# First stage of a gated retention and attention block: half of the modulation summed on VectorE, the keys' banks held open over two chunks

## The chip, the cores and the metric

One NeuronCore of one Trainium2 chip runs the whole block in one launch. The metric is the device time of one execution in microseconds (us). Engines are named as in the profile: PE is TensorE's matrix multiply, PEld its weight load, DVE is VectorE, ACT is ScalarE, POOL is GpSimd, SP issues most of the DMAs.

## The reference, cut to what matters

The block computes, for a sequence of 512 tokens and a model width of 2048:

```
mod = silu(c) @ w_ada + b_ada                      # c: one vector of 2048; w_ada: 2048 x 6144
shift, scl, gate = split(mod, 3)
h = rmsnorm(x) * g_norm * (1 + scl) + shift        # 512 x 2048
(r_q, r_k, r_v, r_g, n_q, n_kc, n_vc, n_ks, ...) = split(h @ w_in)
...
x = rmsnorm(x + gate * (merged @ w_out)) * g_final
```

The keys of the attention half (n_ks, n_kw) and the queries are rotated by position: `x * cos + rot(x) * sin`. Everything behind `h @ w_in` needs h, and h needs the sum over all 2048 rows of `w_ada` for its own columns. The change touches this first stage only.

## The kernel before, in words

The 2048 columns of h are made in eight chunks of 256 (j = 0 to 7, two k-tiles of 128 each). For a chunk the 2 x 256 columns of `w_ada` for shift and scale are loaded as eight items of 512 KB (each holds two k-tiles of the sum). TensorE multiplies them with silu(c): two k-tiles per item, with 32 columns of weights, so that four such products lie side by side in the array (`ada_batch`, L353, output tile `pa`). ScalarE copies the sums to SBUF (`ada_rows`, L358, tile `rows`), four small matmuls turn them into columns (`cols_mm`, L336, tile `misc`), three small VectorE operations make the two factors of each column (tile `sh`, L372 to L374), and `cols_h` applies them: VectorE scales (L381), ScalarE rounds to the high part `hhi` (L382), VectorE takes the rest `hlo` (L383). Every product with h is made of three matmuls (hi x hi, hi x lo, lo x hi), and the weights are split likewise: `whi` on ScalarE (L269), `wlo` on VectorE (L270).

As soon as two k-tiles of h exist, two groups of columns of `w_in` use them: the group "kc" keeps four PSUM banks open over all chunks (class `Group`, L453, tile `g`), 24 matmuls per chunk, and the group "k" (the keys) takes 24 matmuls per chunk in two banks that take turns (`k_step`, L907, tile `g` too); after each chunk VectorE adds every finished bank to an SBUF sum `kacc` (L913). After the last chunk the keys are rotated in place (`rope`, L529 to L533). The position tables cos and sin are made on VectorE in small operations that are spread over the chunks (`rope_tables`, L503 to L522).

The order on each engine is the order of the program text; nothing is moved by a scheduler. Steps of the two groups lie in a list `todo`, and `pop(room)` emits some of them between the modulation's batches. A step can only stand behind the chunk whose k-tiles it reads. `early_splits` splits weights ahead, up to an item that `lim` names. The loads go out on SP in the order of `plan`, each into the next free one of nine slots (seventeen up to chunk 2), and wait there until the slot's last reader is done.

After the first stage the next group is "v" (matmuls of L453 again, between them the products `phid` of the compression, L642), then the queries and the rest of `w_in`.

Of the kernel before, what the change touches and what calls it, by code (L numbers as in the profile page):

```python
# [85 lines left out]
def block_kernel(ctx: ExitStack, tc: tile.TileContext, t_in, out):  # L86
    nc = tc.nc
# [17 lines left out]
    def sbank(name):  # L105
        return bank("pss", 2, name)
# [66 lines left out]

    plan = []


    BATCH = [[2, 2, 2, 2]] * 2 + [[4, 4]] * 6
    for j in range(8):
        for u in range(8):
            plan.append(("a", j, u))  # L180
            if (j, u) == (0, 3):
                plan.append(("w", "in", 0, 0))
        plan += [("w", "in", g, j) for g in range(2) if j or g]
    n_start = len(plan)
    for g in range(2, NG):
        for s in range(8):
# [11 lines left out]
        for s in range(8):  # L198
            plan.append(("w", "out", j, s))

    SRC = {"a": "w_ada", "in": "w_in", "c": "w_c1", "g": "w_gate", "up_r": "w_ur", "up_n": "w_un", "out": "w_o"}
    raws, splits = {}, {}
    loaded = [0]
    w_idx = [i for i, it in enumerate(plan) if it[0] == "w"]
    w_ord = {i: n for n, i in enumerate(w_idx)}
    parked = {}
    split_ptr = [0]
# [44 lines left out]
    def take(i):  # L252

        if i not in raws:
            load(i)
        slots.append(held.pop(i))
        return raws.pop(i)
# [55 lines left out]
    def rstd_rows():  # L313
        prs = sbank("prs")
        for t in range(NT):
            c = slice(t * P, (t + 1) * P)
            nc.tensor.matmul(prs[:, c], ones, rtmp[:, 2, c], start=t == 0, stop=t == NT - 1, skip_group_check=True)
        nc.vector.tensor_copy(rstd, prs)


    def xn(j, us):

        for u in us:
            kk = 2 * j + u
            h = xT[kk // 8][:, kk % 8, :]
            nc.vector.tensor_tensor(h, h, rstd, op=OP.mult)
# [12 lines left out]
    pa = {}  # L339

    def ada_batch(idx, j, s0, n):


        load(idx + n - 1)
        per = 2 if j else 4
        w = 1024 // per
        rs = [take(idx + u).rearrange("p (a b) -> p a b", a=per) for u in range(n)]
        if s0 % (NK // per) == 0:
            pa[j] = tbank(f"pa{j}_{s0}")
        for u in range(per * n):  # L350
            kk = (per * s0 + u) % NK
            m = 32 * (kk % 4)
            nc.tensor.matmul(pa[j][m:m + 32, :w], sc32[:, kk, :], rs[u // per][:, u % per, :],  # L353
                             start=kk < 4, stop=kk >= NK - 4)

    def ada_rows(j, w=512):
        rows = wk.tile([P, 512], F32, tag="p", bufs=3, name=f"rows{j}")
        nc.scalar.copy(rows[:, :w], pa.pop(j)[:, :w])  # L358
        return rows

    def cols_mm(j, rows, us):
# [1 line left out]
        for n, q in enumerate([u + 2 * v for v in range(2) for u in us]):  # L363
            misc_mm(pcol[:, j, q:q + 1], rows[:, n * P:(n + 1) * P], ones[:, 0:1])

    def cols_h(j, us, between=None):

        xn(j, us)
        u0, n = us[0], len(us)
        sh = wk.tile([P, 4], F32, tag="sh", bufs=2, name=f"sh{j}{u0}")  # L370
        k0 = 2 * j + u0
        nc.vector.tensor_tensor(sh[:, 0:n], pcol[:, j, u0:u0 + n], bsh[:, k0:k0 + n], op=OP.add)  # L372
        nc.vector.tensor_tensor(sh[:, 2:2 + n], pcol[:, j, 2 + u0:2 + u0 + n], bsc[:, k0:k0 + n], op=OP.add)
        nc.vector.scalar_tensor_tensor(sh[:, 2:2 + n], sh[:, 2:2 + n], 1.0, gn[:, k0:k0 + n], op0=OP.add, op1=OP.mult)  # L374
        for u in range(n):
            kk = k0 + u
            a, k8 = divmod(kk, 8)
            if h_hi[a] is None:
                h_hi[a], h_lo[a] = bigt("hhi1", F32R), bigt("hlo1", F32R)
            h = xT[a][:, k8, :]  # L380
            nc.vector.tensor_scalar(h, h, sh[:, 2 + u:3 + u], sh[:, u:u + 1], op0=OP.mult, op1=OP.add)  # L381
            nc.scalar.copy(h_hi[a][:, k8, :], h)  # L382
            nc.vector.tensor_tensor(h_lo[a][:, k8, :], h, h_hi[a][:, k8, :].bitcast(F32), op=OP.subtract)  # L383

    gates = cst.tile([P, NT, 24], F32, name="gates")
    gate0 = cst.tile([P, NH], F32, name="gate0")
# [33 lines left out]
    def flush():  # L420
        while side:
            side.popleft()()
# [103 lines left out]
    def rope(dst, src, cs, sn, n, nm, view=lambda a: a):  # L526

        rot = wk.tile([P, n], F32, tag="rot", bufs=1, name=f"rot{nm}")
        nc.scalar.copy(view(rot[0:64]), src[64:128])  # L529
        nc.scalar.copy(view(rot[64:128]), src[0:64])  # L530
        nc.vector.tensor_tensor(dst, src, cs, op=OP.mult)
        nc.vector.tensor_tensor(view(rot), view(rot), sn, op=OP.mult)
        nc.vector.tensor_tensor(dst, dst, view(rot), op=OP.add)  # L533
# [362 lines left out]
    g0 = Group("F", [gbank(f"g0_{t}") for t in range(4)], hhi, hlo, NK, evac_in(0))  # L896
    kacc = [ev_tile(f"kacc{t}") for t in range(4)]

    def k_step(i, n, t):

        whi, wlo = splits[i]
        b = sbank(f"g1_{t}_{n}")
        for u in range(2):
            kk = 2 * n + u
            f = slice(u * 512 + t * P, u * 512 + t * P + P)
            for m, (l, r) in enumerate(((whi[:, f], hhi(kk)), (whi[:, f], hlo(kk)), (wlo[:, f], hhi(kk)))):
                nc.tensor.matmul(b, l, r, start=u == 0 and m == 0, stop=u == 1 and m == 2)  # L907
        if t == 3:
            splits.pop(i)
        if n == 0:  # L910
            nc.scalar.copy(kacc[t], b)
        elif n < 7:
            nc.vector.tensor_tensor(kacc[t], b, kacc[t], op=OP.add)  # L913
        else:
            if t == 0:
                res["kT"] = kvp.tile([P, 4, 512], F32, tag="kv", name="kT")
            nc.vector.tensor_tensor(kacc[t], b, kacc[t], op=OP.add)
            rope(res["kT"][:, t, :], kacc[t], cosT, sinT, 512, f"k{t}")

    idx = 0  # L920
    todo = deque()
    tables = deque(rope_tables())

    lim = [0]

    def early_splits():
# [1 line left out]
        while len(splits) < 3 and w_idx[split_ptr[0]] < min(loaded[0], lim[0]):  # L928
            split(split_ptr[0])

    def queue_item(i, us=None):

        it = plan[i]
        if it[2] == 0:
            todo.extend((6 if us is None else 3, f) for f in g0.steps([i], us))
        else:
            todo.extend((6, lambda t=t: k_step(i, it[3], t)) for t in range(4))
# [12 lines left out]
    for b in range(2):  # L950
        ada_batch(2 * b, 0, 2 * b, 2)
# [2 lines left out]
    split(0, part)  # L954
    cols_mm(0, rows, (0,))
    rstd_rows()
    cols_h(0, (0,))
    part[0]()
    queue_item(i_w0, (0,))
    ada_batch(5, 0, 4, 2)  # L960
    pop(6)
    ada_batch(7, 0, 6, 2)
# [1 line left out]
    pop(6)  # L964
    cols_mm(0, rows, (1,))
    cols_h(0, (1,))
    queue_item(i_w0, (1,))
    queue_item(9)
    idx = lim[0] = 10
    for j in range(1, 8):  # L970
        if j == 2:
            for dst, src in late:
                nc.sync.dma_start(dst, src)
        s0 = 0
        nb = len(BATCH[j])
        for b, n in enumerate(BATCH[j]):
            load(idx)
            ada_batch(idx, j, s0, n)
            idx += n
            s0 += n  # L980
            if b == nb - 1:
                rows = ada_rows(j)
                lim[0] = idx + 1
            pop(24 // nb if j == 1 else 48 // nb if b < nb - 1 else 42 // nb - 6)
            for _ in range(2):
                if j > 2 and tables:
                    tables.popleft()()
        pop(6)
        cols_mm(j, rows, (0, 1))
        cols_h(j, (0, 1))  # L990
        for i in (idx, idx + 1):
            queue_item(i)
        idx += 2
        lim[0] = idx
    gates_finish = None
    while tables:
        tables.popleft()()
    i = 0
    while todo:
        load(idx - 2)  # L1000
        early_splits()
        todo.popleft()[1]()
        i += 1
        if i == 4:
            gates_finish = make_gates()
        if i == 8:
            gates_finish()
    comp = lambda i, it: comp_slice(i, it[1], it[2])
    for g in range(2, NG):
        name, kind, _ = GROUPS[g]  # L1010
        bk = [gbank(f"g{g}_{t}") for t in range(4)]
        idx = run_group(Group(kind, bk, hhi, hlo, NK, evac_in(g)), idx, 8, comp)
# [227 lines left out]
```

## Time and profile before

| | us |
|---|---|
| median of 3 runs | 1632.57 (1632.54 to 1633.15) |
| the profiled execution | 1637.63 |
| its span in the trace | 1635.8 |
| TensorE busy in the span | 1591.5 (97%) |
| VectorE busy | 720.1 (44%) |
| ScalarE busy | 496.1 (30%) |

The profiled execution took 5.1 us longer than the median of the runs, and 1.8 us of its time lie outside the span. Busy TensorE time is that of overlapping matmuls, so that it overstates how full the engine is.

### The profile page before, as it was taken

How to read it: one execution, taken by the hardware profiler on the slowest of the kernel's cores; microseconds unless marked ns; L12 is line 12 of the kernel's file. 1: busy time of each engine (PE TensorE's matmuls, PEld its weight loads, DVE VectorE, ACT ScalarE, POOL GpSimd, SP SyncE). 2: the span in 40 equal slices, each digit the busy share in tenths (PEclk: the TensorE clock that was granted, in tenths of full speed). 3: DMA queues.
4: the chain of work that ended last, by engine and by line, in shares of the span. 5: the costliest groups of instructions: out<-in, count | busy, mean ns of one | idle time of the engine just before them, and what ended most of it. 6: DMA issues, size and time to landing. Idle time of an engine off the chain costs nothing.

```text
span 1635.8 us, 18919 instructions
## 1 busy us (share of the span) xinstructions
PE 1591.5 (97%) x7518; PEld 1268.9 (78%) x7518; DVE 720.1 (44%) x1253; ACT 496.1 (30%) x732; POOL 28.1 (2%) x57
## 2 busy tenths in 40 slices
PE   5999899999999999999999999999999999999997
PEld 2565577888888888788888888888888878878886
DVE  4465532455444435533244443332222566754444
ACT  3212212343333534432233333332222222222223
POOL 0000000000000000000000100000001000010000
PEclk9999799999999999999999999999999999999999
DMA  9985145323233223222534645333335767785322
GB/s 339 352 309 206 65 149 184 125 90 104 71 110 104 91 65 98 74 86 91 161 114 162 195 140 184 119 121 107 115 121 174 246 230 245 261 286 198 97 84 103
DMA packets 96857, 252.55 MB, mean 154 GB/s; under 512 B 10448, under 2 KB 28032, under 8 KB 95616
## 3 DMA queue, kind: packets, MB, share of 16 engines
q1 hardware_dynamic: 89184, 236.62, 43.0%
q0 software_dynamic: 7008, 12.61, 2.5%
q10 hardware_dynamic: 576, 2.10, 0.3%
q8 instruction: 59, 0.97, 0.2%
q14 instruction: 30, 0.25, 0.0%
HBM read 224.03 MB, written 27.26 MB: 154 GB/s over the span
## 4 chain that ended last, share of the span: by engine, by line
PE 85%; DVE 7%; ACT 3%; DMA 3%; issue 2%; SPq 0%; ACTq 0%; DVEq 0%
PE g L453 57%; PE o L453 10%; PE u L453 5%; PE o L758 2%; PE sc L721 2%; PE g L907 1%; DVE wlo L270 1%; PE tp L744 1%; DMA raw<-in_w_ur 1%; PE pa L353 1%; PE phid L642 1%; PE ssq L288 1%; DMA raw<-in_w_un 1%; DVE hlo L383 1%; ACT hhi L382 1%
## 5 line engine op out<-in xcount | busy, mean ns | idle before, releaser
L270 DVE TENSOR_TENSOR wlo<-raw,whi 128x1024 fp32r<-128x1024 f32 x240 | 290.7, 1223 | 510.1 <-ACT whi L269 506.5
L453 PE MATMUL g<-hhi,whi 128*128 128x512 f32 x1088 | 439.8, 404 | 6.4 <-ACT hhi L382 6.4
L453 PE MATMUL g<-hlo,whi 128*128 128x512 f32 x1088 | 426.9, 392 | 2.3 <-DVE hlo L383 2.0
L453 PE MATMUL g<-hhi,wlo 128*128 128x512 f32 x1088 | 425.9, 391 | 2.3 <-DVE wlo L270 2.3
L269 ACT CAST whi<-raw 128x1024 fp32r<-128x1024 f32 x240 | 249.0, 1048 | 499.7 <-PE g L453 244.3
L453 PEld LDWEIGHTS g<-hhi,whi 128*128 128x128 f32 x1088 | 205.1, 189 | 63.4 <-ACT hhi L382 11.1
L453 PEld LDWEIGHTS g<-hlo,whi 128*128 128x128 f32 x1088 | 205.3, 189 | 49.7 <-DVE hlo L383 7.2
L453 PEld LDWEIGHTS g<-hhi,wlo 128*128 128x128 f32 x1088 | 205.1, 188 | 46.8 <-DVE wlo L270 3.4
L453 PE MATMUL g<-whi,hhi 128*128 128x512 f32 x320 | 135.2, 422 | 3.2 <-ACT whi L269 3.2
L453 PE MATMUL g<-wlo,hhi 128*128 128x512 f32 x320 | 125.9, 393 | 0.9 <-DVE wlo L270 0.9
L453 PE MATMUL g<-whi,hlo 128*128 128x512 f32 x320 | 126.0, 394 | 0.0
L453 PE MATMUL o<-whi,mhi 128*128 128x512 f32 x240 | 95.0, 396 | 0.0
L453 PE MATMUL o<-wlo,mhi 128*128 128x512 f32 x240 | 93.6, 390 | 0.3 <-DVE wlo L270 0.3
L453 PE MATMUL o<-whi,mlo 128*128 128x512 f32 x240 | 93.4, 389 | 0.0
L453 PEld LDWEIGHTS g<-whi,hhi 128*128 128x128 f32 x320 | 60.8, 190 | 19.8 <-ACT whi L269 5.1
L453 PEld LDWEIGHTS g<-wlo,hhi 128*128 128x128 f32 x320 | 60.9, 190 | 16.8 <-issue 2.4
L453 PEld LDWEIGHTS g<-whi,hlo 128*128 128x128 f32 x320 | 60.6, 189 | 13.3
L724 DVE CUSTOM_DVE_ANT_0 p<-sc,c_mask 128x128 f32<-128x128 f32 (+3 forms) x64 | 31.2, 487 | 85.3 <-PE sc L721 85.2
L745 ACT COPY pT<-tp 128x128 f32<-128x128 f32 (+3 forms) x64 | 27.2, 426 | 114.6 <-PE tp L744 114.4
L726 ACT ACTIVATE p<-p,sm 128x128 f32<-128x128 f32 (+3 forms) x64 | 36.0, 563 | 75.6 <-DVE sm L724 75.6
L453 PEld LDWEIGHTS o<-wlo,mhi 128*128 128x128 f32 x240 | 45.0, 188 | 10.9 <-issue 1.0
L758 PEld LDWEIGHTS o<-pT,vt 128*128 128x128 f32 x320 | 44.8, 190 | 10.9 <-issue 5.3
(238 smaller groups left out, 1728.0 us busy)
## 6 DMA issues: line engine op xcount, KB each, us to landing
raw<-in_w_in SPq DMA_DIRECT2D x178, 512.0 KB, 3.7
raw<-in_w_gate SPq DMA_DIRECT2D x32, 512.0 KB, 5.1
raw<-in_w_o SPq DMA_DIRECT2D x32, 512.0 KB, 4.4
raw<-in_w_ada SPq DMA_DIRECT2D x26, 512.0 KB, 6.3
xkv<-in_w_ada SPq DMA_DIRECT2D x21, 512.0 KB, 6.8
raw<-in_w_c SPq DMA_DIRECT2D x16, 512.0 KB, 4.4
raw<-in_w_un SPq DMA_DIRECT2D x16, 512.0 KB, 5.4
sg<-ma_d SPq DMA_DIRECT2D x32, 256.0 KB, 3.4
```

Of the source, the lines that this page charges most:

```text
L269: nc.scalar.copy(hi, r)
L270: low = lambda hi=hi, lo=lo, r=r: nc.vector.tensor_tensor(lo, r, hi.bitcast(F32), op=OP.subtract)
L288: nc.tensor.matmul(ssq, ones, sq[u], start=a == 0 and u == 0, stop=a == 3 and u == 2)
L353: nc.tensor.matmul(pa[j][m:m + 32, :w], sc32[:, kk, :], rs[u // per][:, u % per, :], start=kk < 4, stop=kk >= NK - 4)
L382: nc.scalar.copy(h_hi[a][:, k8, :], h)
L383: nc.vector.tensor_tensor(h_lo[a][:, k8, :], h, h_hi[a][:, k8, :].bitcast(F32), op=OP.subtract)
L453: nc.tensor.matmul(self.banks[t], l, r, start=kk == 0 and n == 0, stop=kk == self.nk - 1 and n == 2)
L721: nc.tensor.matmul(b[:, :n], qT[:, h, t], res["kT"][:, 2 * br + g, :n], start=True, stop=True)
L724: nc.vector.tensor_tensor_reduce(p[:, :n], b[:, :n], mask[:, 512 - n:], -SCALE, 3.0e38, OP.add, OP.min, sm[:, 0:1])
L726: nc.scalar.activation(p[:, :n], p[:, :n], AF.Exp, bias=sm[:, 0:1], scale=-1.0, accum_out=sm[:, 1:2])
L745: nc.scalar.copy(pT[:, :n], b[:, :n])
L758: nc.tensor.matmul(o[:, r * P:(r + 1) * P], res["v"][:, m, 256 * br + P * g:256 * br + P * g + P], pT[:, m * P:(m + 1) * P], start=k == fi ...
```

## The change

In chunks 1 to 7 the first four of the eight `w_ada` items are summed on VectorE (`ada_vec`: one multiplication and seven multiply-adds into the tile `av`), and only the last four go through TensorE, in one batch. `ada_rows` is then the VectorE sum of both halves. The high part of h and the scaled value are both made on ScalarE from the normalised x, with scale and bias, so that the scaling on VectorE goes; the normalisation (`xn`) is written further ahead. The keys' weights are loaded in another cut (`w_half`: half of the columns, four k-tiles), so that a key bank stays open over two chunks, and `kacc` is added to half as often. The position tables and the rotation of the keys are written behind the first stage, among the steps of the groups "v" and "nq0".

```diff
+        plan.append(("h", j % 2, j // 2))
...
+        first = s0 % (NK // per) == (0 if j == 0 else 4)
...
+    def ada_vec(idx, j, u):
+        load(idx)
+        r = take(idx).rearrange("p (a b) -> p a b", a=2)
+        for v in range(2):
+            kk = 2 * u + v
+            if kk == 0:
+                av[j] = wk.tile([P, 512], F32, tag="p", bufs=3, name=f"av{j}")
+                nc.vector.tensor_scalar(av[j], r[:, v, :], sc[:, kk:kk + 1], None, op0=OP.mult)
+            else:
+                nc.vector.scalar_tensor_tensor(av[j], r[:, v, :], sc[:, kk:kk + 1], av[j], op0=OP.mult, op1=OP.add)
...
     def ada_rows(j, w=512):
         rows = wk.tile([P, 512], F32, tag="p", bufs=3, name=f"rows{j}")
-        nc.scalar.copy(rows[:, :w], pa.pop(j)[:, :w])
+        if j:
+            nc.vector.tensor_tensor(rows, pa.pop(j), av.pop(j), op=OP.add)
...
-            nc.vector.tensor_scalar(h, h, sh[:, 2 + u:3 + u], sh[:, u:u + 1], op0=OP.mult, op1=OP.add)
-            nc.scalar.copy(h_hi[a][:, k8, :], h)
+            nc.scalar.activation(hi, h, AF.Identity, scale=sh[:, 2 + u:3 + u], bias=sh[:, u:u + 1])
+            nc.scalar.activation(h, h, AF.Identity, scale=sh[:, 2 + u:3 + u], bias=sh[:, u:u + 1])
...
+        rooms = [0, 6, 6, 6, 6, 0, 0] if j == 1 else [6, 6, 6, 6, 6, 6, 6]
+        rooms[4] += 6 * (j % 2 == 0)
+        rooms[5] += 6 * (j % 2 == 0)
+        pop(rooms[6])
+        for u in range(4):
+            ada_vec(idx + u, j, u)
+            pop(rooms[u])
+        xn(j, (0, 1))
+        idx += 4
+        ada_batch(idx, j, 4, 4)
+        idx += 4
+        pop(rooms[4])
+        rows = ada_rows(j)
+        lim[0] = idx + 1
+        pop(rooms[5])
         cols_mm(j, rows, (0, 1))
         cols_h(j, (0, 1))
+        lim[0] = idx + 2
+        if j % 2:
+            queue_k(i_h, (2, 3), (0, 1))
+            queue_w(idx)
+            queue_k(idx + 1, (0, 1, 2, 3), (2, 3))
+        else:
+            i_h = idx + 1
+            queue_k(i_h, (0, 1), (0, 1))
+            queue_w(idx)
...
+    lim[0] = len(plan)
...
+    side.extend(rope_tables() + [lambda t=t: k_rope(t) for t in range(4)])
+    rate[0] = 0.45
```

What stands on TensorE behind the four `misc` matmuls of a chunk is the first place to look at (names end in a buffer's number; `g_..` at L907 or L929 is a bank of the keys). Before, behind chunk 3:

```order
L907 MATMUL g_2_2_623<-hhi_189,wlo_546 128x512
L336 MATMUL misc<-ones,rows_593 128x1 [waits Activation_49]
L336 MATMUL misc<-ones,rows_593 128x1 x3
L353 MATMUL pa_0_653<-raw_579,rtmp 32x512 [waits DMAHW0_49,PE_49]
L353 MATMUL pa_0_653<-raw_579,rtmp 32x512
L353 MATMUL pa_0_653<-raw_581,rtmp 32x512 [waits DMAHW1_49]
```

Now, behind chunk 4 (an even one):

```order
L929 MATMUL g_3_1_726<-hhi_189,wlo_629 128x512
L337 MATMUL misc<-ones,rows_720 128x1 [waits DVE_49]
L337 MATMUL misc<-ones,rows_720 128x1 x3
L929 MATMUL g_0_2_760<-hhi_748,whi_756 128x512 [waits Activation_49]
L929 MATMUL g_0_2_760<-hlo_749,whi_756 128x512 [waits DVE_49]
L929 MATMUL g_0_2_760<-hhi_748,wlo_757 128x512 [waits DVE_49]
```

Half a batch of the modulation and one key step stood between `misc` and the first matmul on the new k-tiles; now that matmul follows at once.

The second place is ScalarE at the end of the same chunk 4, in the kernel after the change (`whi_722` belongs to "kc", `whi_756` to the keys):

```order
L270 CAST whi_722<-raw_645 128x1024 [waits DMAHW0_49,PE_49]
L399 ACTIVATE hhi_748<-xT_80,sh_744 128x512 [waits DMAHW4_49,DMAHW5_49,DMAHW3_49,DVE_49]
L400 ACTIVATE xT_80<-xT_80,sh_744 128x512 [waits Activation_49]
L399 ACTIVATE hhi_748<-xT_80,sh_744 128x512
L400 ACTIVATE xT_80<-xT_80,sh_744 128x512 [waits Activation_49]
L270 CAST whi_756<-raw_657 128x1024 [waits DMAHW1_49,PE_49]
```

The split of the keys' weights, which the first three matmuls behind `misc` read, stands behind the four activations of the new k-tiles.

The third place is VectorE at the end of the first stage. Before:

```order
L405 TENSOR_SCALAR gate_193<-gates,c_valid_96 128x8 [waits Activation_49]
L917 TENSOR_TENSOR kacc_204<-g_3_7_1237,kacc_204 128x512 [waits PE_49]
L531 TENSOR_TENSOR kT<-kacc_204,cosT 128x512 [waits DVE_49]
L532 TENSOR_TENSOR rotk_1245<-rotk_1245,sinT 128x512 [waits Activation_49]
L533 TENSOR_TENSOR kT<-kT,rotk_1245 128x512 [waits DVE_49]
L270 TENSOR_TENSOR wlo_1257<-raw_1118,whi_1256 128x1024 [waits DMAHW0_49,Activation_49]
```

Now:

```order
L271 TENSOR_TENSOR wlo_1079<-raw_1009,whi_1078 128x1024 [waits DMAHW7_49,Activation_49]
L937 TENSOR_TENSOR kacc_201<-g_0_3_982,kacc_201 128x512 [waits PE_49]
L937 TENSOR_TENSOR kacc_202<-g_1_3_1002,kacc_202 128x512 [waits PE_49]
L271 TENSOR_TENSOR wlo_1101<-raw_1068,whi_1100 128x1024 [waits DMAHW0_49,Activation_49]
L564 COPY kcT<-g_0_196 128x512 [waits PE_49]
L564 COPY kcT<-g_1_197 128x512 [waits PE_49]
```

The first weights of the group "v" (`wlo_1257` before, `wlo_1101` now) were split behind the four rotations of the keys; they are now split ahead of them, while TensorE still has steps of the first stage.

## Rows read from the trace of the kernel before

**Rows 1.** Busy time by stage: the chunks 1 to 7, then their end.
```profile
core 0: us, PE busy (x) PEld busy (x) DVE busy (x) ACT busy (x) POOL busy (x), PEclk, DMA share, GB/s
...
39.00:157.40 118.40, 113.89 (x605) 71.50 (x604) 67.21 (x119) 30.13 (x41) 0.00 (x0) 1.00 0.83 306
157.40:189.00 31.60, 22.12 (x89) 13.67 (x89) 18.95 (x29) 11.84 (x17) 0.00 (x0) 0.76 0.06 17
```

**Rows 2.** Chain that ended last, first stage: start us, us, what.
```profile
40.11 0.62 ACT hhi L382
...
88.42 0.63 ACT hhi L382
...
91.66 3.51 PE g L453 x14
95.17 1.85 PE pa L353 x16
...
105.64 0.63 ACT hhi L382
...
157.94 0.63 ACT hhi L382
```

**Rows 3.** Groups by line and form: busy us, mean ns; idle before.
```profile
L269 ACT CAST whi<-raw 128x1024 fp32r<-128x1024 f32 x240 | 249.0, 1048 | 499.7 <-PE g L453 244.3 <-PE o L453 72.5 <-DMA raw<-in_w_in 51.0
L382 ACT CAST hhi<-xT 128x512 fp32r<-128x512 f32 x16 | 9.9, 619 | 58.9 <-DVE xT L381 58.9
L843 ACT ACTIVATE ro<-ro,c_xi 128x512 f32<-128x512 f32 x8 | 5.5, 688 | 28.2 <-PE ro L840 23.4 <-DMA raw<-in_w_in 4.8
...
L270 DVE TENSOR_TENSOR wlo<-raw,whi 128x1024 fp32r<-128x1024 f32 x240 | 290.7, 1223 | 510.1 <-ACT whi L269 506.5 <-DMA raw<-in_w_in 3.6
L383 DVE TENSOR_TENSOR hlo<-xT,hhi 128x512 fp32r<-128x512 f32 x16 | 11.1, 692 | 11.0 <-ACT hhi L382 11.0
L381 DVE TENSOR_SCALAR xT<-xT,sh 128x512 f32<-128x512 f32 x16 | 8.7, 544 | 0.3
L503 DVE SCALAR_TENSOR_TENSOR rtmp<-rtmp 128x512 f32<-128x512 f32 x6 | 4.1, 687 | 0.1
```

**Rows 4.** Timeline around two `misc` groups: start us, us, engine, line, what.
```profile
38.53 0.50 PE L336 MATMUL misc<-ones,rows 128*128 128x1 f32 x4
39.07 0.16 DVE L372 TENSOR_TENSOR sh<-misc,c_bsh 128x1 f32<-128x1 f32 x1 [5.16 <-PE misc L336]
39.53 0.55 DVE L381 TENSOR_SCALAR xT<-xT,sh 128x512 f32<-128x512 f32 x1
...
102.57 0.95 PE L336 MATMUL misc<-ones,rows 128*128 128x1 f32 x8
```

**Rows 5.** Chain that ended last, end of the first stage and first steps of "v".
```profile
160.45 6.87 PE g L453 x15
167.32 3.57 PE pbg L394 x32
...
173.88 0.70 DVE kacc L917
...
187.74 1.23 DVE wlo L270
189.02 13.41 PE g L453 x47
202.43 1.88 PE phid L642 x16
204.30 11.10 PE g L453 x48
```

**Rows 6.** DMA issues, first 190 us: KB each, median us to landing.
```profile
raw<-in_w_ada SPq DMA_DIRECT2D x26, 512.0 KB, 6.3
```

**Rows 7.** Windows around three stretches with little TensorE work; columns as in rows 1.
```profile
29.40:33.80 4.40, 1.48 (x8) 0.75 (x5) 3.65 (x8) 0.62 (x1) 0.00 (x0) 1.00 1.02 407
33.80:37.20 3.40, 3.40 (x21) 1.38 (x20) 0.12 (x1) 0.17 (x1) 0.00 (x0) 0.50 1.04 412
...
157.20:160.10 2.90, 1.38 (x4) 0.48 (x3) 1.82 (x4) 0.94 (x2) 0.00 (x0) 1.00 0.00 0
160.10:166.90 6.80, 6.45 (x15) 4.75 (x15) 2.52 (x3) 1.25 (x2) 0.00 (x0) 0.50 0.27 80
...
88.40:92.00 3.60, 3.00 (x12) 1.72 (x10) 1.99 (x4) 2.19 (x3) 0.00 (x0) 1.00 0.77 245
```

More of the change, by code (lines that the diff above doesn't have):

```diff
@@ L174, in block_kernel @@
     plan = []
-    BATCH = [[2, 2, 2, 2]] * 2 + [[4, 4]] * 6
     for j in range(8):
@@ L182, in block_kernel @@
                 plan.append(("w", "in", 0, 0))
-        plan += [("w", "in", g, j) for g in range(2) if j or g]
+        if j:
+            plan.append(("w", "in", 0, j))
+        plan.append(("h", j % 2, j // 2))
     n_start = len(plan)
@@ L199, in block_kernel @@
             plan.append(("w", "out", j, s))
-    SRC = {"a": "w_ada", "in": "w_in", "c": "w_c1", "g": "w_gate", "up_r": "w_ur", "up_n": "w_un", "out": "w_o"}
+    SRC = {"a": "w_ada", "h": "w_half", "in": "w_in", "c": "w_c1", "g": "w_gate", "up_r": "w_ur", "up_n": "w_un", "out": "w_o"}
     raws, splits = {}, {}
     loaded = [0]
-    w_idx = [i for i, it in enumerate(plan) if it[0] == "w"]
+    w_idx = [i for i, it in enumerate(plan) if it[0] in "wh"]
     w_ord = {i: n for n, i in enumerate(w_idx)}
@@ L347, in ada_batch @@
         rs = [take(idx + u).rearrange("p (a b) -> p a b", a=per) for u in range(n)]
-        if s0 % (NK // per) == 0:
+        first = s0 % (NK // per) == (0 if j == 0 else 4)
+        if first:
             pa[j] = tbank(f"pa{j}_{s0}")
@@ L353, in ada_batch @@
             nc.tensor.matmul(pa[j][m:m + 32, :w], sc32[:, kk, :], rs[u // per][:, u % per, :],
-                             start=kk < 4, stop=kk >= NK - 4)
+                             start=first and u < 4, stop=kk >= NK - 4)
+    av = {}
+    def ada_vec(idx, j, u):
[8 more added lines that the diff above has]
+                nc.vector.scalar_tensor_tensor(av[j], r[:, v, :], sc[:, kk:kk + 1], av[j], op0=OP.mult, op1=OP.add)
     def ada_rows(j, w=512):
         rows = wk.tile([P, 512], F32, tag="p", bufs=3, name=f"rows{j}")
-        nc.scalar.copy(rows[:, :w], pa.pop(j)[:, :w])
+        if j:
+            nc.vector.tensor_tensor(rows, pa.pop(j), av.pop(j), op=OP.add)
+        else:
+            nc.scalar.copy(rows[:, :w], pa.pop(j)[:, :w])
         return rows
@@ L364, in cols_mm, with cols_h @@
             misc_mm(pcol[:, j, q:q + 1], rows[:, n * P:(n + 1) * P], ones[:, 0:1])
-    def cols_h(j, us, between=None):
-        xn(j, us)
+    def cols_h(j, us):
         u0, n = us[0], len(us)
@@ L371, in cols_h @@
         k0 = 2 * j + u0
-        nc.vector.tensor_tensor(sh[:, 0:n], pcol[:, j, u0:u0 + n], bsh[:, k0:k0 + n], op=OP.add)
         nc.vector.tensor_tensor(sh[:, 2:2 + n], pcol[:, j, 2 + u0:2 + u0 + n], bsc[:, k0:k0 + n], op=OP.add)
         nc.vector.scalar_tensor_tensor(sh[:, 2:2 + n], sh[:, 2:2 + n], 1.0, gn[:, k0:k0 + n], op0=OP.add, op1=OP.mult)
+        nc.vector.tensor_tensor(sh[:, 0:n], pcol[:, j, u0:u0 + n], bsh[:, k0:k0 + n], op=OP.add)
         for u in range(n):
@@ L379, in cols_h @@
                 h_hi[a], h_lo[a] = bigt("hhi1", F32R), bigt("hlo1", F32R)
-            h = xT[a][:, k8, :]
-            nc.vector.tensor_scalar(h, h, sh[:, 2 + u:3 + u], sh[:, u:u + 1], op0=OP.mult, op1=OP.add)
-            nc.scalar.copy(h_hi[a][:, k8, :], h)
-            nc.vector.tensor_tensor(h_lo[a][:, k8, :], h, h_hi[a][:, k8, :].bitcast(F32), op=OP.subtract)
+            h, hi = xT[a][:, k8, :], h_hi[a][:, k8, :]
+            nc.scalar.activation(hi, h, AF.Identity, scale=sh[:, 2 + u:3 + u], bias=sh[:, u:u + 1])
+            nc.scalar.activation(h, h, AF.Identity, scale=sh[:, 2 + u:3 + u], bias=sh[:, u:u + 1])
+            nc.vector.tensor_tensor(h_lo[a][:, k8, :], h, hi.bitcast(F32), op=OP.subtract)
     gates = cst.tile([P, NT, 24], F32, name="gates")
@@ L897, in block_kernel, with k_step @@
     kacc = [ev_tile(f"kacc{t}") for t in range(4)]
-    def k_step(i, n, t):
+    kb = {}
+    def k_step(i, n, t, us):
         whi, wlo = splits[i]
[L902 to L905, printed above, removed]
+        if us[0] == 0:
+            kb[t] = sbank(f"g1_{t}_{n}")
+        b = kb[t]
+        for u in us:
+            kk = 4 * n + u
+            f = slice(u * 256 + (t % 2) * P, u * 256 + (t % 2) * P + P)
             for m, (l, r) in enumerate(((whi[:, f], hhi(kk)), (whi[:, f], hlo(kk)), (wlo[:, f], hhi(kk)))):
-                nc.tensor.matmul(b, l, r, start=u == 0 and m == 0, stop=u == 1 and m == 2)
-        if t == 3:
+                nc.tensor.matmul(b, l, r, start=u == 0 and m == 0, stop=u == 3 and m == 2)
+        if us[-1] < 3:
+            return
+        if t % 2:
             splits.pop(i)
@@ L911, in k_step, with k_rope @@
             nc.scalar.copy(kacc[t], b)
-        elif n < 7:
+        else:
             nc.vector.tensor_tensor(kacc[t], b, kacc[t], op=OP.add)
[L914 to L918, printed above, removed]
+    def k_rope(t):
+        if t == 0:
+            res["kT"] = kvp.tile([P, 4, 512], F32, tag="kv", name="kT")
+        rope(res["kT"][:, t, :], kacc[t], cosT, sinT, 512, f"k{t}")
     idx = 0
     todo = deque()
-    tables = deque(rope_tables())
     lim = [0]
@@ L929, in early_splits, with queue_w, queue_k @@
             split(split_ptr[0])
[L931 to L937, printed above, removed]
+    def queue_w(i, us=None):
+        todo.extend((6 if us is None else 3, f) for f in g0.steps([i], us))
+    def queue_k(i, us, ts):
+        n = plan[i][2]
+        todo.extend((3 * len(us), lambda t=t: k_step(i, n, t, us)) for t in ts)
     def pop(room):
@@ L948, in block_kernel @@
     i_w0 = plan.index(("w", "in", 0, 0))
+    i_h = plan.index(("h", 0, 0))
     load(0)
@@ L956, in block_kernel @@
     rstd_rows()
+    xn(0, (0,))
     cols_h(0, (0,))
     part[0]()
-    queue_item(i_w0, (0,))
+    xn(0, (1,))
+    queue_w(i_w0, (0,))
     ada_batch(5, 0, 4, 2)
@@ L966, in block_kernel @@
     cols_h(0, (1,))
-    queue_item(i_w0, (1,))
-    queue_item(9)
-    idx = lim[0] = 10
+    queue_w(i_w0, (1,))
+    queue_k(i_h, (0, 1), (0, 1))
+    idx = lim[0] = i_h + 1
     for j in range(1, 8):
@@ L973, in block_kernel @@
                 nc.sync.dma_start(dst, src)
[L974 to L988, printed above, removed]
+        rooms = [0, 6, 6, 6, 6, 0, 0] if j == 1 else [6, 6, 6, 6, 6, 6, 6]
[13 more added lines that the diff above has]
+        pop(rooms[5])
         cols_mm(j, rows, (0, 1))
         cols_h(j, (0, 1))
-        for i in (idx, idx + 1):
-            queue_item(i)
+        lim[0] = idx + 2
[3 more added lines that the diff above has]
+            queue_k(idx + 1, (0, 1, 2, 3), (2, 3))
+        else:
+            i_h = idx + 1
+            queue_k(i_h, (0, 1), (0, 1))
+            queue_w(idx)
         idx += 2
-        lim[0] = idx
+    lim[0] = len(plan)
     gates_finish = None
-    while tables:
-        tables.popleft()()
     i = 0
@@ L1003, in block_kernel @@
         i += 1
-        if i == 4:
+        if i == 3:
             gates_finish = make_gates()
-        if i == 8:
+        if i == 6:
             gates_finish()
+    side.extend(rope_tables() + [lambda t=t: k_rope(t) for t in range(4)])
+    rate[0] = 0.45
     comp = lambda i, it: comp_slice(i, it[1], it[2])
@@ L1013, in block_kernel @@
         if name == "nq0":
+            flush()
             side.extend(comp_finish())
```

## The prediction

> **What bounds the kernel now.** I read the busy time by stage first, then the chain that ended last over the first 200 us, then the windows with their granted clock. Chunks 1 to 7 lie between the first activation on new k-tiles of chunk 0 (40.11) and that of chunk 7 (157.94) [rows 2]: seven turns of 16.8 us. In one turn (88.42 to 105.64, 17.2 us) TensorE works off 48 matmuls, two half batches of the modulation at 1.85 and the small `misc` group at 0.95 [rows 2, 4]. A matmul in a dense row costs 11.10 / 48 = 0.231 [rows 5], so that this is 11.1 + 3.7 + 0.95 = 15.75 us; the other 1.4 us are waits for `hhi` and `hlo`. The turn is thus nearly full on TensorE, while VectorE is busy for 67 of 118 us and the DMA share is 0.83 at 306 GB/s [rows 1]. After chunk 7 this ends: from 157.4 to 189 TensorE is partly idle and at a mean clock of 0.76 [rows 1]. The chain goes there through the rotation of the keys on VectorE (from 173.88), behind which the first `wlo` of "v" waits until 187.74 [rows 5]. After that TensorE is dense again, which is where a gain or loss made earlier is carried to the end.
>
> **What the change does to a turn.** TensorE loses one half batch, 1.85 us a turn. VectorE gains the sum of four items: 0.54 for the multiplication (as L381) and seven dependent multiply-adds at 0.69 plus a hand-over of some 0.02 (as L503), 5.4 us, and 0.69 for the sum of both halves; it loses two scalings (1.1), two of four additions to `kacc` (1.4) and the tables [rows 3]. That keeps it under a turn's length. The turn is then set by what follows `misc`, so I walk through it, from A, the start of the first `hhi` activation. An activation with scale and bias isn't in the trace; its bounds are 0.62 (L382) and 0.69 (L843) [rows 3], and I take 0.65, as it reads SBUF like the first.
>
> Of A itself: from the first of the three small `sh` operations to the operation that needs them all pass 0.46, and `sh` starts 0.04 after `misc` ends (39.03) [rows 4]. So A is 0.5 after `misc`. ScalarE then makes `hhi` 0 (to 0.65), the scaled x 0 (to 1.33), `hhi` 1 (to 1.91), x 1 (to 2.6); VectorE makes `hlo` 0 (to 2.05) and `hlo` 1 (to 3.3).
>
> After an odd chunk the first key step has its weights already: its matmuls run at 0.7 (`hhi` 0), 2.1 (`hlo` 0), 2.3, 2.5, and the fifth waits for `hlo` 1, A + 3.34. Then 26 matmuls (6.0), one batch (1.85), 30 matmuls (6.9), `misc` (0.95) and 0.5 to the next A: 19.6 us. After an even chunk the first step needs key weights whose `whi` stands behind the four activations: 1.05 [rows 3], to A + 3.55; its `wlo` takes 1.22 [rows 3], to A + 4.8. The third matmul starts there; 28 matmuls (6.5), a batch (1.85), 6 matmuls (1.4), `misc` and 0.5: 16.0 us. Two turns take 35.6 us, against 2 x 17.2 now. The 3.7 us that TensorE saves in two turns go into waits of 2.9 (odd) and 4.8 us (even) behind `misc`, where a half batch and a key step used to stand. VectorE is ready in time: after an even chunk its sum is done at 4.8 + 5.4 + 1.4 = 11.6 and the batch at 13.2; after an odd one some 14 against a bank that comes at 15.7.
>
> Chunk 1 has only 24 matmuls and one new k-tile ahead of it: `hlo` at 2.05, VectorE's sum with one `wlo` and the normalisation to 10.6, `misc`, 0.5: 12.1 us. With A of chunk 0 at 39.6 (the scaling of 0.55 on VectorE is gone from its chain [rows 4]), A of chunk 7 falls on 39.6 + 12.1 + 3 x 35.6 = 158.5, where it is 157.94 now [rows 2].
>
> Loads: an item of a chunk goes into the slot that was freed nine items before. The tightest is the last item of TensorE's batch after an odd chunk: its slot is freed by the `wlo` at A + 4.8, it is read at about A + 10.3, and landing takes 6.3 in the median [rows 6]. That is 0.8 late at most in three turns, 2.4 us; a lone load lands sooner than this median of a busy queue, so I take 0.
>
> **The end of the stage.** From A of chunk 7: the fifth matmul at 3.34, 56 matmuls 12.9, the gate product `pbg` 3.57 [rows 5], its four small matmuls about 1.1 (estimated from `misc`), and "v" begins at A + 20.95 = 179.45, since its `wlo` now lies ahead of `kacc` and no rotation stands on VectorE. Its first 48 matmuls take 11.1 and end at 190.55; now they end at 202.43 [rows 5]. That is 11.9 us gained: the way from A of chunk 7 to there shrinks from 44.5 to 32.05 us, and the chunks give back 0.6.
>
> The rotations (12 operations of 0.69) and 18 table operations go among "v" and "nq0", about one for two of the steps of six matmuls. TensorE is dense there (11.10, then 1.88, then on [rows 5]) and VectorE gets one operation between two `wlo`s: hidden, 0. If none were hidden it would be some 18 us; nothing in that stage speaks for it.
>
> **The clock.** What is not yet in the sum is what TensorE does after the waits. Twice in the trace a stretch with few matmuls was followed by the 1.2 GHz level: 29.4 to 33.8 (1.48 of 4.4 us busy), then 0.50 for 3.4 us; 157.2 to 160.1 (1.38 of 2.9), then 0.50 for 6.8 us. 88.4 to 92.0, with 3.0 of 3.6 busy, stayed at 1.00 [rows 7]. The second is the wait of an odd end almost matmul for matmul (`hhi`, `hlo`, `wlo`, next `hhi`), and there 15 matmuls took 6.87 where 14 take 3.51 [rows 2, 5]: 3.1 lost. A dip of 3.4 us over dense work costs 1.7. I take 2.2 for one, as part of it lies on idle time. The wait after an even chunk, from the start of `misc`, is 6.2 us long with two matmuls in it: emptier than either stretch, so I count a dip at all three. After an odd chunk it is 4.8 us with four matmuls: I count two of four. That is 5 x 2.2 = 11.0 us.
>
> The Trainium skill has a rule on this (TensorE: Matmul & The Clock Gate, section "HAM oscillation — how this bites in real kernels"): a loop that lets the array wait in every turn falls back to half rate in every turn and pays the way up each time. The trace agrees in direction (the two dips above); by that rule all seven ends dip, 15.4 us instead of 11.0, and the sum would end 3.5 us above the time before.
>
> **Sum.** -11.9 + 11.0 = -0.9: 1636.7 for an execution like the profiled one (1637.63), and against the median of the runs, 5.1 lower, 1632.57 - 0.9 = 1631.7. About 0.2% (3.3 us) is what a measurement of this kernel can tell from no change.
>
> **Rivals.**
> - *Dips after the even chunks only* (3 x 2.2 = 6.6): -5.3, 1627.3. For it: the odd ends keep four matmuls and `misc` in the wait. Against it: the stretch at 157.2.
> - *No dips*: -11.9, 1620.7. For it: the clock stayed at 1.00 through all seven turns before. Against it: those turns had 1.4 us of waits each, and now it is 2.9 and 4.8.
> - *TensorE's saving is kept*: no wait behind `misc`, a turn of 48 x 0.231 + 1.85 + 0.95 + 0.5 = 14.4 us, seven of them from 39.6 end at 140.4, another 18.1 us: 1602.6. For it: the turn before is nearly full of TensorE work. Against it: the order, in which nothing stands behind `misc`.
> - *Slower: a dip at every end*, seven of them at 2.2 to 3.1, mean 2.6: 18.2 - 11.9 = +6.3, 1638.9. For it: the stretch at 157.2 and its long dip. It decides from (11.9 + 3.3) / 7 = 2.2 us a dip on. The rule of the Trainium skill that is named above leads here too.
>
> **How the numbers follow.** Forecast 0.38, even ends only 0.25, no dips 0.13, saving kept 0.04, a dip at every end 0.20. The forecast's own spread (a dip more or less, 0.65 to 0.69 for an activation, 2.4 us for loads) is about 4 us either way. The range 1620 to 1640 leaves out the kept saving, about half of the case without dips and a third of the slower one: some 0.17. Faster by over 0.2%: 0.07 of the forecast's 0.38, 0.18 of the even ends, 0.13 and 0.04: 0.42. Slower: 0.07 of the forecast and 0.16 of the slower case: 0.23. The rest, 0.35, is within 0.2%.
>
> **What would show it.** In the changed kernel's profile: turns of about 19.6 (to an even end) and 16.0 us (to an odd end), without the dips; TensorE idle for about 3.9 us behind `misc` of chunks 2, 4 and 6, released by ScalarE's `whi` and VectorE's `wlo`; granted clock 0.50 for 3 to 7 us behind those; the first matmul of "v" near 180 plus the dips; "v" and "nq0" as dense as before. The prediction is wrong if the clock stays at 1.00 behind the even ends, if VectorE's sum is late for `misc`, or if a load holds TensorE's batch.

## The result and the profile after

The change makes the kernel slower: 1644.41 us in the median of six runs (1642.96 to 1645.68), against 1633.09 for the kernel before, also over six runs; ratio 1.0066, 95% interval 1.0053 to 1.0079. The forecast was 1631.7, its range ended at 1640, and its slower rival stood at 1638.9. Medians are over the runs that agree; one run of the kernel called cover 18 and 30 below took 2510.52 us at a granted clock of 0.591 and is left out.

The windows of the kernel after, as in [rows 1, 7]. The first seven are the stretches behind the ends of chunks 1 to 7, the eighth is all six turns between them, the last the rest of the program from the end of the first 48 matmuls of "v".

```profile
core 0: us, PE busy (x) PEld busy (x) DVE busy (x) ACT busy (x) POOL busy (x), PEclk, DMA share, GB/s
53.00:59.20 6.20, 5.62 (x13) 4.07 (x14) 5.02 (x7) 4.04 (x6) 0.00 (x0) 0.50 0.92 334
77.00:83.30 6.30, 5.34 (x12) 3.76 (x13) 5.88 (x8) 0.86 (x1) 0.00 (x0) 0.50 0.26 83
94.00:100.60 6.60, 5.53 (x13) 4.01 (x13) 5.13 (x7) 3.70 (x5) 0.00 (x0) 0.50 0.47 166
118.00:124.60 6.60, 5.44 (x12) 3.86 (x13) 6.01 (x8) 1.07 (x2) 0.00 (x0) 0.50 0.44 129
135.00:141.20 6.20, 5.22 (x12) 3.66 (x12) 4.67 (x6) 3.80 (x5) 0.00 (x0) 0.50 0.45 158
159.00:165.30 6.30, 5.09 (x11) 3.63 (x12) 5.67 (x8) 1.12 (x2) 0.00 (x0) 0.50 0.40 117
176.00:182.30 6.30, 5.37 (x12) 3.64 (x12) 4.35 (x5) 3.98 (x6) 0.00 (x0) 0.50 0.31 92
...
50.90:174.50 123.60, 102.22 (x432) 71.96 (x432) 74.96 (x117) 32.72 (x40) 0.00 (x0) 0.83 0.68 243
...
209.20:1642.10 1432.90, 1418.99 (x6671) 1163.41 (x6670) 625.59 (x1076) 447.08 (x664) 25.54 (x48) 1.00 0.42 140
```

The granted clock is at 0.50, the 1.2 GHz level, behind all seven ends, four odd and three even. Before, the turns ran at 1.00 throughout. VectorE's busy time, 74.96 of 123.6 us, leaves it free enough, and the last row (1432.9 us; 1433.4 before, from 202.43 on) says that nothing is lost later: the loss is in the first stage.

What the engines wait for in these turns (the view of waits from 51 to 175: engine, line and releaser, us in all, times, longest):

```profile
PE g L929 <- ACT whi L270: 14.1, 3, 4.7
...
DVE rows L375 <- PE pa L355: 11.2, 4, 3.6
...
PE g L929 <- ACT hhi L399: 4.1, 3, 1.4
PE g L929 <- DVE hlo L401: 3.1, 3, 1.1
```

TensorE waits for the new k-tiles and the split keys' weights, as walked through in the forecast. VectorE waits for TensorE's half of the modulation, not the other way round. The timeline around the end of chunk 4:

```profile
113.48 0.95 PE L337 MATMUL misc<-ones,rows 128*128 128x1 f32 x8
...
114.66 0.16 DVE L391 SCALAR_TENSOR_TENSOR sh<-sh,c_gn 128x2 f32<-128x2 f32 x1
...
114.92 0.81 ACT L399 ACTIVATE hhi<-xT,sh 128x512 fp32r<-128x512 f32 x1 [10.17 <-DVE sh L392]
...
117.32 0.81 ACT L400 ACTIVATE xT<-xT,sh 128x512 f32<-128x512 f32 x1
118.04 1.03 ACT L270 CAST whi<-raw 128x1024 fp32r<-128x1024 f32 x1
...
119.10 1.23 DVE L271 TENSOR_TENSOR wlo<-raw,whi 128x1024 fp32r<-128x1024 f32 x1 [0.24 <-ACT whi L270]
...
119.12 0.80 PE L929 MATMUL g<-hhi,whi 128*128 128x512 f32 x1 [4.70 <-ACT whi L270]
...
120.38 0.80 PE L929 MATMUL g<-hhi,wlo 128*128 128x512 f32 x1
```

TensorE does nothing from 114.43 to 119.12, and starts again at half clock. The chain of the work that ended last, answering to [rows 2, 5], names a load here. But the cast at 118.04 follows straight behind the fourth activation (117.32 + 0.81 = 118.13), and the view of waits has the same 4.7 us behind all three even ends (14.1 in 3 times), so the load is not what held it:

```profile
92.64 0.82 ACT hhi L399
...
95.08 5.34 PE g L929 x11
...
113.40 4.66 DMA raw<-in_w_ada
118.05 1.03 ACT whi L270
...
120.38 4.51 PE g L929 x10
...
174.76 0.82 ACT hhi L399
...
184.04 3.57 PE pbg L412 x32
...
198.33 10.88 PE g L471 x48
209.20 1.88 PE phid L660 x16
```

Eleven matmuls take 5.34 us, where a dense row would take 2.5. And the groups that were new (by line and form: busy us, mean ns; idle before), answering to [rows 3]:

```profile
L370 DVE SCALAR_TENSOR_TENSOR av<-raw,sc,av 128x512 f32<-128x512 f32 x26 | 19.5, 751 | 0.8
...
L400 ACT ACTIVATE xT<-xT,sh 128x512 f32<-128x512 f32 x16 | 13.0, 814 | 0.5
L399 ACT ACTIVATE hhi<-xT,sh 128x512 fp32r<-128x512 f32 x16 | 12.9, 807 | 79.9 <-DVE sh L392 79.9
```

An activation with scale and bias takes 0.81 us, outside the forecast's bounds of 0.62 and 0.69.

### The profile page after: what moved, and what is told of

The parts are those of the page before. It is cut to its first block, busy times and chain, and to the rows that moved or that the text cites. A ratio compares the mean times of both kernels' runs of the same rounds, so it can differ in the third digit from the quotient of the medians.

```text
span 1642.1 us, 18759 instructions
## 1 busy us (share of the span) xinstructions
PE 1584.2 (96%) x7406; PEld 1274.3 (78%) x7406; DVE 745.5 (45%) x1284; ACT 506.9 (31%) x741; POOL 28.0 (2%) x57
## 4 chain that ended last, share of the span: by engine, by line
PE 91%; DVE 4%; DMA 2%; ACT 2%; issue 1%; SPq 0%; DVEq 0%; ACTq 0%
PE g L471 58%; PE o L471 10%; PE u L471 7%; PE g L929 3%; PE o L776 2%; PE sc L739 2%; PE tp L762 1%; DVE wlo L271 1%; PE phid L660 1%; PE pa L355 1%; DMA raw<-in_w_ur 1%; PE ssq L289 1%; DMA raw<-in_w_ada 1%; PE o L773 1%; DMA raw<-in_w_o 0%
## 5 line engine op out<-in xcount | busy, mean ns | idle before, releaser
L471 PEld LDWEIGHTS g<-whi,hhi 128*128 128x128 f32 x320 | 60.1, 188 | 15.6 <-issue 2.1
L471 PEld LDWEIGHTS o<-whi,mhi 128*128 128x128 f32 x240 | 45.1, 188 | 10.3 <-issue 1.0
```

Source lines behind the costliest of these rows:

```text
L471: nc.tensor.matmul(self.banks[t], l, r, start=kk == 0 and n == 0, stop=kk == self.nk - 1 and n == 2)
```

## The experiments

Two theories of the miss. **Clock and wait apart:** the empty stretch behind `misc` costs once as a wait, as long as the way from `sh` to the last `hlo` or `wlo`, and a second time as seven dips of the clock. **Rivals:** VectorE's sum or the loads set the turn; or the clock only shows the wait and costs nothing of its own. A turn is measured below from one chunk's `sh` operation with `c_gn` to the next one's (114.66 in the timeline above; the second of the three in the changed kernel, the third in the kernel before), as the profiles give it:

| kernel | median us | behind odd chunk 3 | behind even chunk 4 |
|---|---|---|---|
| before, second profile | 1634.42 | 17.2 | 17.7 |
| after | 1644.41 | 22.3 | 18.8 |
| tail alone | 1620.89 | 17.2 | 17.1 |
| old scaling | 1641.88 | 22.4 | 18.8 |
| even split | 1637.64 | 23.0 | 15.8 |
| filled wait | 1631.49 | 20.4 | 16.9 |
| filled, two scalings | 1620.62 | 19.1 | 15.4 |
| cover 18 and 24 | 1617.95 | 16.8 | 15.8 |
| cover 18 and 30 | 1616.50 | 15.5 | 16.4 |
| cover 18 and 30, two scalings | 1607.99 | 15.6 | 15.0 |

**The kernel before again**, no edit.

> The kernel before, unchanged, profiled a second time. Its first profile was 5.1 us above the median of its runs (1637.63 against 1632.57) and had the granted clock at 0.50 for 6.8 us behind the last chunk. If that dip belongs to the order of the kernel, this profile has it again; if it comes and goes, the profiled time is near 1633 and the stretch behind the last chunk stays at 1.00 or dips elsewhere. Time 1633 +- 1 either way.

Measured: 1634.42 (ratio 1.0001, 0.9992 to 1.0011), a profiled span of 1631.9 in place of 1635.8. The window that stands at 0.50 for its whole 6.8 us in [rows 7]:

```profile
160.10:166.90 6.80, 6.42 (x28) 4.10 (x31) 2.52 (x3) 1.34 (x2) 0.00 (x0) 0.75 0.26 80
```

Both executions dip here, but this time it lasted half as long. From the chain, to be read beside [rows 5]:

```profile
160.55 5.48 PE g L453 x15
...
187.73 12.63 PE g L453 x47
200.36 1.88 PE phid L642 x16
```

The `phid` behind the first 48 matmuls of "v" started at 200.36, 2.1 us earlier than in the first profile: the 15 matmuls behind the dip took 5.48 us in place of 6.87, and the first 47 of "v" 12.63 in place of 13.41. The forecast took all of the first profile's end as what the change removes; these 2 us another execution doesn't have.

**The tail alone**, in the kernel before:

```diff
-            for _ in range(2):
-                if j > 2 and tables:
-                    tables.popleft()()
...
-    while tables:
-        tables.popleft()()
+    lim[0] = len(plan)
...
+    side.extend(rope_tables() + [lambda t=t: k_rope(t) for t in range(4)])
+    rate[0] = 0.45
```

> The kernel before with one part of the change alone: tables and key rotations written among v and nq0, and the first weights of v split ahead of the last kacc. The forecast's term for the end of the stage was -11.9: 1621 (1619 to 1624), v's first 48 matmuls ending near 190 in place of 202.4, dense as before. Rival: the moved VectorE work shows among v and nq0 (up to 18 us): 1633 or more.

Measured: 1620.89, ratio 0.9919 (0.9904 to 0.9934), 13.0 us faster. From its chain:

```profile
176.63 10.89 PE g L453 x48
187.52 1.88 PE phid L642 x16
189.40 11.10 PE g L453 x48
```

The tables and rotations run up to 257 us in this trace, among the steps of "v", and they cost nothing that shows: from the first `phid` to the end it is 1431.9 us, against 1431.5 in the second profile of the kernel before. The rest of the change, all of it inside the first stage, thus loses 1644.4 - 1620.9 = 23.5 us.

**The old scaling**, in the kernel after:

```diff
-            nc.scalar.activation(hi, h, AF.Identity, scale=sh[:, 2 + u:3 + u], bias=sh[:, u:u + 1])
-            nc.scalar.activation(h, h, AF.Identity, scale=sh[:, 2 + u:3 + u], bias=sh[:, u:u + 1])
+            nc.vector.tensor_scalar(h, h, sh[:, 2 + u:3 + u], sh[:, u:u + 1], op0=OP.mult, op1=OP.add)
+            nc.scalar.copy(hi, h)
```

> The changed kernel with the scaling as before (VectorE scales, ScalarE rounds): ScalarE has two casts of 0.62 in the place of four activations of 0.81 ahead of the key weights' split. Theory (empty waits): the third matmul behind an even misc starts 1.3 us earlier, the fifth behind an odd one 0.2 us earlier, all ends still dip: 1639 to 1641. Rival (the long activations make the odd ends dip): the odd ends stay at 1.00 as well, another 4 x 2.1 us: 1630 to 1633.

Measured: 1641.88 (ratio 1.0041, 1.0026 to 1.0055); turns and dips as in the kernel after. The median is 2.5 us below the changed kernel's, but the profiled execution (1643.67, the longest of five) doesn't show where. The saving of 1.3 us that I expected isn't there, as the timeline of its chunk 4 shows:

```profile
116.06 0.55 DVE L399 TENSOR_SCALAR xT<-xT,sh 128x512 f32<-128x512 f32 x1
...
117.90 0.54 DVE L399 TENSOR_SCALAR xT<-xT,sh 128x512 f32<-128x512 f32 x1
118.47 0.62 ACT L400 CAST hhi<-xT 128x512 fp32r<-128x512 f32 x1 [1.22 <-DVE xT L399]
119.00 1.04 ACT L270 CAST whi<-raw 128x1024 fp32r<-128x1024 f32 x1
```

I had overlooked that the second scaling stands behind the first `hlo` on VectorE, which waits for ScalarE: the two engines take turns, and the chain is nearly as long as that of the four activations (`whi` starts 3.2 us behind the `sh` operation at 115.80, 3.4 in the changed kernel).

**The keys' weights split earlier at the even ends**, in the kernel after:

```diff
-        lim[0] = idx + 1
+        lim[0] = idx + 1 + (j % 2 == 0)
```

> The changed kernel with the split of the key weights let in one step earlier at the even chunks, ahead of the four activations. Theory: the even ends then wait like the odd ones, for the second hlo (4.0 us from the first activation) and not for wlo (5.5), but still dip: 3 x 1.3 to 1.5 = 4 to 4.5 us, 1640. Rival (the even ends' longer wait is what brings the dip there): three dips less as well, 1633.

Measured: 1637.64 (1.0029, 1.0017 to 1.0040), 6.8 us less than the kernel after, between the two expectations. Two of its windows, behind chunks 4 and 6:

```profile
112.60:119.00 6.40, 4.16 (x10) 2.71 (x11) 3.67 (x8) 3.15 (x4) 0.00 (x0) 0.73 0.44 168
...
150.80:158.00 7.20, 4.97 (x11) 3.37 (x12) 4.45 (x9) 3.15 (x4) 0.00 (x0) 0.64 0.53 196
```

The even ends still dip, for a shorter time, and their turns shrink by 1.7 to 3.0 us.

**The wait filled with matmuls that nobody reads**, in the kernel after:

```diff
         cols_h(j, (0, 1))
+        for _ in range((20, 12)[j % 2]):
+            nc.tensor.matmul(misc[:, 32:], h_hi[0][:, 0, :P], h_hi[0][:, 1, 32:], start=False, stop=False,
+                             skip_group_check=True)
```

> The changed kernel with 12 (odd chunks) or 20 (even chunks) extra matmuls of 480 columns behind misc, on old k-tiles into unused columns of the misc bank; nobody reads them, so the output is unchanged, and TensorE does 108 more matmuls of 0.22 us. They fill 2.6 and 4.3 us from the sh operations on, no more than the wait itself. Theory (waits and clock apart): the waits for hlo and wlo end when they did, but the clock stays at 1.00: seven dips of 2.15 us are saved, 1629 to 1631, with a pair of turns at 41.2 - 4.3 = 36.9. Rival (the clock is not what costs, the waits alone are): 1643 or, with the added work, up to 1650.

Measured: 1631.49, ratio 0.9989 (0.9979 to 0.9999), 12.9 us less than the kernel after although TensorE does 108 matmuls more. One window over the last six ends (the clock is at 1.00 behind chunk 1 too), and the matmuls behind the end of chunk 4 in the timeline:

```profile
70.00:180.00 110.00, 105.04 (x530) 77.00 (x529) 71.89 (x111) 33.96 (x40) 0.00 (x0) 1.00 0.68 237
```

```profile
110.64 4.54 PE L1018 MATMUL misc<-hhi 128*128 128x480 f32 x20 [0.52 <-DVE sh L392]
...
116.11 0.50 PE L929 MATMUL g<-hhi,wlo 128*128 128x512 f32 x1 [0.46 <-DVE wlo L271]
```

The `wlo` is waited for as before (the matmul at 116.11 starts 5.75 us behind the second `sh` operation, 5.72 in the changed kernel), but at a clock of 1.00. This separates the two: the clock costs 12.9 us (13.5 if each median is taken against the kernel before of its own session), 1.8 to 1.9 a dip. The other 1631.5 - 1620.9 = 10.6 is what the longer waits cost beyond the TensorE work that is saved; the tail alone, the measure here, still has one dip of its own behind chunk 7 (0.74 from 158.5 to 165).

**The same with two scalings one behind the other**, 6 and 14 extra matmuls:

```diff
-            nc.scalar.activation(hi, h, AF.Identity, scale=sh[:, 2 + u:3 + u], bias=sh[:, u:u + 1])
-            nc.scalar.activation(h, h, AF.Identity, scale=sh[:, 2 + u:3 + u], bias=sh[:, u:u + 1])
+            nc.vector.tensor_scalar(h, h, sh[:, 2 + u:3 + u], sh[:, u:u + 1], op0=OP.mult, op1=OP.add)
+            nc.scalar.copy(hi, h)
+        for u in range(n):
...
             nc.vector.tensor_tensor(h_lo[a][:, k8, :], h, hi.bitcast(F32), op=OP.subtract)
...
+        for _ in range((14, 6)[j % 2]):
```

> The run with extra matmuls behind misc (1631.5, clock 1.00), and in it two scalings on VectorE and two casts on ScalarE in the place of the four activations; 6 and 14 extra matmuls in place of 12 and 20. Theory (at full clock the length of a turn is the way from sh to the last hlo or wlo, and the rest of the forecast's miss is the size of the four activations): from the rows of the run with 30 kept back and two scalings, the second hlo is ready 2.8 us behind the start of the second sh operation in place of 4.2, and wlo 4.2 in place of 5.7: 4 x 1.4 + 3 x 1.5 = 10 us less, 1620 to 1623. Rival (the activations are off the path, loads or VectorE's sum hold the turn): 1629 to 1632.

Measured: 1620.62, ratio 0.9918 (0.9901 to 0.9934): 10.9 us less, the clock at 1.00 in windows behind each end. At full clock the chain from `sh` is what sets the turn.

**Cover: old steps kept behind `misc`**, in the kernel after, first 18 matmuls at odd and 24 at even ends, then 18 and 30, then 18 and 30 with the two scalings:

```diff
-        rooms[4] += 6 * (j % 2 == 0)
-        rooms[5] += 6 * (j % 2 == 0)
+        if j > 2 and j % 2:
+            rooms = [6, 0, 0, 6, 6, 0, 6]
...
-        pop(rooms[5])
+        while sum(n for n, f in todo) > (24, 18)[j % 2] * (j > 1):
+            pop(1)
```

> The changed kernel, but 18 (odd chunks) or 24 (even chunks) matmuls of the last queued steps are kept back and stand behind misc. Theory (empty waits): the new k-tiles and key weights are made behind 4.2 and 5.5 us of TensorE work, the granted clock stays at 1.00, and a pair of turns shrinks from 41.2 us towards its TensorE work of 27.8: 10 to 13 us a pair, three pairs, and 4 us at the end: 1603 to 1612. Rival (VectorE's sum or late loads set the turn): the wait only moves ahead of misc, where rows or raw is late, and the time stays at 1638 to 1645.

> As the run that kept 18 and 24 matmuls back (1618.0), with 30 at the even chunks in place of 24, so that the two turns of a pair have 48 matmuls each in place of 42 and 54. In that run VectorE's sum was 1.6 us late for the misc of the odd chunks and the clock fell to 0.50 behind it. Theory: TensorE's turn of 48 x 0.231 + 1.85 + 0.95 = 13.9 us leaves a wait of about 1 us for VectorE there, and two or three of the dips go: 1611 to 1615. Rival (VectorE alone sets that turn): 1617 to 1619.

> As the run with 30 and 18 kept back, and in the place of the four activations two scalings on VectorE, one behind the other, and two casts on ScalarE. Theory: the second hlo is ready some 3.1 us behind sh in place of 4.4, and VectorE, which waits idle for 2.5 us in each turn between the four activations, gets its sum done 1 us earlier in the turns that it limits: 1608 to 1612. Rival: the 1.1 us of scalings that VectorE takes back cancel it: as the run with 30.

Measured: 1617.95 (0.9900, 0.9885 to 0.9915), 1616.50 (0.9904, 0.9877 to 0.9932) and 1607.99 (0.9850, 0.9829 to 0.9870). The first recovers 26.5 us of the kernel after, but not the 32 and more that I expected. Its timeline at the end of chunk 5 shows the next limit:

```profile
116.05 0.68 DVE L375 TENSOR_TENSOR rows<-pa,av 128x512 f32<-128x512 f32 x1
...
116.79 1.05 PE L337 MATMUL misc<-ones,rows 128*128 128x1 f32 x8 [1.64 <-DVE rows L375]
```

In the turns behind even chunks VectorE's sum is now late for `misc`, and a shorter dip follows (0.90 over the next turn). More TensorE work in that turn (30) gains little, 1.5 us. The clock stays at 1.00 from chunk 2 on, as the theory had it, but the time comes out near the rival's, since now an addition to `kacc` behind VectorE's multiply-adds holds a bank. From its chain in the turn behind chunk 4:

```profile
111.35 0.75 DVE av L370
112.10 0.61 DVE kacc L937
...
112.76 1.66 PE g L929 x6
```

So with the clock back, VectorE's chain still sets this turn. Shortening VectorE's idle time between the activations does. A window over one turn of the last kernel, its shortest (the others take 14.4 to 15.6):

```profile
111.60:125.90 14.30, 14.30 (x74) 10.37 (x73) 13.53 (x22) 3.26 (x4) 0.00 (x0) 1.00 0.98 371
```

TensorE, VectorE and the DMA queues are all nearly full there. This version is 25.7 us faster than the kernel before and 36.4 faster than the changed one. Against the tail alone (1620.9) the new first stage gains 12.9 us in it, and 2.9 and 4.4 in the two kernels before it; whether the old first stage with two scalings in a row would do as well was not tried.

## Why the prediction was wrong

- **The end of the stage, -11.9: right.** The tail alone gave -13.0, of which 11.1 lie behind chunk 7 (200.36 - 157.27 in the second profile of the kernel before, 187.52 - 155.49 now). Without a dip the way from the last chunk's second `sh` operation to the end of "v"'s first 48 matmuls took 197.46 - 164.54 = 32.9 us in the filled kernel, against 32.05 + 0.26 forecast, the 0.6 by the activations.
- **That the waits stand behind `misc`, VectorE in time, no load late, side work hidden: right**, by the views of waits and windows after.
- **"I count two of four": this step failed.** All four odd ends dipped, so that seven dips stood in place of five. The price, 2.2 taken and 1.8 to 1.9 measured, was somewhat high and made up for part of the count. In all 12.9 (or 13.5) in place of 11.0. The evidence was in the forecast: the stretch at 157.2 is an odd end "almost matmul for matmul", and it dipped; counting half of its like had no row behind it. The rule of the Trainium skill (TensorE: Matmul & The Clock Gate, section "HAM oscillation — how this bites in real kernels"), by which all seven dip as the forecast applied it, agrees with the seven windows at 0.50. The section's own example has one unbroken wait in each turn, as the even ends have (4.7 us); the odd ends, where no single wait for `hhi` or `hlo` is over 1.4 us, dipped as well.
- **The activation, 0.65 in bounds of 0.62 and 0.69: the larger miss.** At 0.81 the fifth matmul after an odd chunk starts 3.99 us behind A (96.63 - 92.64) in place of 3.34, the third after an even one 5.46 (120.38 - 114.92) in place of 4.8. With the clock at 1.00 the turns took 20.4 and 16.9 us, forecast 19.6 and 16.0. Turns, chunk 1 (12.7, forecast 12.1) and the end were 6.3 us longer than forecast; 7 x 0.65 = 4.6 of it is this chain, the rest, some 0.2 a turn, was not taken apart. The bounds came from a cast (0.62) and from an activation with scale alone (0.69, and it reads PSUM); neither had a bias, and no row showed an operation with both.
- **The base, a term of its own.** The sum was made against one profiled execution, and then 5.1 us were taken off because that execution lay so much above the median. But 2.1 us of this lay in the stretch that the change removes, so that they were taken off twice, in the -11.9 and here. Another 1.8 lay behind the stage, which took 1433.4 us in the first profile and 1431.5 in the second.
- **A reading that the sum doesn't use:** "the other 1.4 us are waits for `hhi` and `hlo`" is too much. From 87 to 157 in the kernel before TensorE waited 2.6 us for them, 0.65 a turn.

By the two profiled executions the account closes. The changed kernel's took 1643.87, where 1636.7 was forecast for one like the first profile: 7.2 us more. The dips are 2.5 of it (13.5 between the traces of the changed and the filled kernel, against 11.0) and the longer turns and end 6.3 (from chunk 0 to chunk 7 the filled kernel took 124.6, forecast 118.9, and 0.6 more at the end); chunk 0 was done 1.2 us earlier than forecast, and the rest of the program took 0.5 less. The other 5.5 of the 12.7 us missed are the base: the 5.1 taken off, and 0.5 by which the changed kernel's median lies above its profiled execution. The slower rival named the right count of dips, but at 2.6 us each and without the longer chain, so that it too fell short.

## What to carry to other kernels

When work is taken off a busy engine, look at what then stands behind its next dependency: here 1.85 us less TensorE work in a turn turned into an empty wait, paid once as time and again as clock. Keep independent steps behind a short dependent group, just enough to cover the chain that makes its successors' operands, and measure wait and clock apart by filling the gap with matmuls that nobody reads. A count of clock dips should follow the one stretch of the trace that has the same shape. And a profile that lies above the median of its runs is no offset to take off: look first which stretch the excess lies in.

## What the runs showed of the hardware

- ScalarE's activation with scale and bias from `sh` on 128x512 in SBUF took 0.81 us, where the plain cast took 0.62 and an activation from PSUM with scale alone 0.69; VectorE's dependent multiply-add with a column as scalar took 0.75, where the one with a constant took 0.69.
- The same wait in two executions of one kernel was followed by 0.50 for 6.8 us in one and a mean of 0.75 in the other; the 15 matmuls at the start of that window took 6.87 and 5.48 us.
- 108 more matmuls behind the waits' start made the kernel 12.9 us faster: the waits ended when they had ended before, and the granted clock stayed at 1.00.
- Two short waits with matmuls between them, none over 1.4 us, were followed by 0.50 at all four odd ends, as the single wait of 4.7 us was at the three even ones.
